# A one-layer decoder kernel: early gates, top-16 steps, piecewise reads, V's first block and the last run rearranged

## The chip, the cores and the metric

The kernel runs on one core of a Trainium2 chip. The core has a matmul engine (TensorE, PE in the profile, with its weight loads as PEld), a vector engine (DVE), an activation engine (ACT), GpSimd (POOL) and a queue engine (SP). DMAs are issued from SP and POOL here. Each engine works through its own list of instructions in order and waits on semaphores. The metric is the device time of one execution in microseconds (us). A profile is one execution with the hardware profiler on; its span runs from the first to the last instruction, and the execution's own time is a little longer.

## The reference

One decoder layer on 256 tokens of width 2048, in f32: two kinds of attention side by side, attention into 256 memory tokens, a layer of single-neuron experts chosen by product keys (PEER), and a last RMS norm. The change touches the PEER layer and the last norm:

```python
def peer_ffn(hn, w_pq, sub_keys, u_tab, v_tab):
    q = (hn @ w_pq).reshape(T, PEER_HEADS, 2, PEER_D_KEY // 2)      # 8 heads, 2 halves of 128
    s = jnp.einsum('thpd,hpkd->thpk', q, sub_keys)                  # 128 keys per half
    top_s, top_i = lax.top_k(s, 16)
    cand = top_s[:, :, 0, :, None] + top_s[:, :, 1, None, :]
    best_s, best_c = lax.top_k(cand.reshape(T, PEER_HEADS, 256), 16)
    expert = ia * 128 + ib                                          # one of 16384
    gate = jax.nn.softmax(best_s, axis=-1)
    a = jnp.einsum('td,ted->te', xt, u_tab[expert])
    hidden = gate * jax.nn.gelu(a)
    return jnp.einsum('te,ted->td', hidden, v_tab[expert])
...
h = h + peer_ffn(rmsnorm(h, norm_ffn), ...)
y = rmsnorm(h, norm_final)
```

## The kernel before

**Precision.** A weight tile `raw` (128 x 1024, 512 KB, four buffers) comes in over SP. ACT rounds it to `hi` and DVE computes the rest, `lo` (`parts`, L71 and L73). A block of weights (`fm_block`) is two such halves; for each PE runs 8 matmuls with `hi` and 8 with `lo`.

**Order.** The program is written in Python as one long list. A planner then orders each engine's instructions by a simulated time line, so an instruction can move ahead of others where its inputs seem ready. `add_manual_dep` ties an instruction behind another; `self.last_lo` is the latest `lo` in program order.

**Queries (`peer`).** For 8 heads, two weight blocks each (numbered 0 to 15 as `2 * h + p2`) give the queries. `sk`, a head's sub keys, are read over SP, `whole`, the tokens in f32, over POOL from the scratch tensor `hres` ahead of the loop; ACT scales `whole` and DVE norms it in four pieces (blocks 5 to 13). The last query block uses `whole` itself.

**Top-16 steps.** For each head and each half of 128 tokens, `topk_pieces` makes three steps (`keys`; `pairs` and `gate`; `ids` and `sums`), 48 in all. The third appends 16 table writes to `puts` (L1009): POOL scatters 128 gates at a time into a dense table of 128 x 128 x 256 gates in DRAM. Six steps are popped in the query loop. The others are popped beside chunks of U, one a chunk, but none at chunk 0 and at every fifth (`while pieces`). `some(4)` issues up to four waiting writes after each query block or chunk.

**U chunks.** 128 chunks of 128 experts each: PE multiplies, `join` adds the two halves, ACT applies gelu. A chunk's result lies in `self.buf` (`hb`). Chunks from `first` on multiply their gates at once (L814); their gates are read into `hb` eight chunks at a time. For the earlier ones gates are read later, four chunks at a time, into a tile `gates` that takes one of the four `raw` buffers (`table_read`, L797); DVE multiplies one chunk on (L757) and counts signs (L824). A read of the table waits for all table writes. `end` is the chunk at which the last write is placed; the early reads begin at `end + 5`, one a chunk.

**Lists and V.** Experts with one token, few tokens or many are told apart by the counts; ranks within a class are matmuls with small 0/1 matrices (`lists`: `totals` L854, `ranks` L862 and L863); POOL writes hidden rows into lists in DRAM (L892). This is done in two parts (chunks 0 to 83, and the rest). `v_phase` runs over 88 blocks of 128 listed experts: POOL gathers their rows of V (L1060), `hi` and `lo` are made as above (`scaled`, L80 and L82, for experts of one token), and `products` (L1089) adds into `out[tb][q]`, eight PSUM banks: two halves of 128 tokens, four column blocks. `plan` mixes wide blocks (FEW, ALL) with thin ones (ONE) into five runs. A FEW block has 12 matmuls, an ALL block 24, a ONE block 8. After the third run comes a rarely taken branch (`rest`, L1254), then the fourth run (one ALL block) and the last.

**The end.** `square` (L1208) sums squares of a column block, `gained` (L1212) multiplies it with the last gain, `root` takes the inverse root (L163 to L168, L1216, L1217) and `finish` scales (L1227, L1229) and stores. For the first half of the tokens these stand as steps in the last run, for the second behind it.

Of the kernel before, what the change touches and what calls it, by code (L numbers as in the profile page):

```python
# [28 lines left out]
D = 2048  # L29
# [23 lines left out]
class Layer:  # L53
# [595 lines left out]
    def peer(self):  # L649
        nc, tc, a = self.nc, self.tc, self.a  # L650
        with ExitStack() as es:
# [3 lines left out]
            self.total = [ba.tile([128, 128], F32, name="total%d" % tb) for tb in range(2)]  # L655
# [4 lines left out]
            self.listing = False  # L660
# [7 lines left out]
            with ExitStack() as e2:  # L668
                ps = self.ps = e2.enter_context(tc.tile_pool(name="ups", bufs=2, reuse_waits="tile", space=bass.MemoryType.PSUM))
                pieces = []  # L670
                with tc.tile_pool(name="tk", bufs=1, reuse_waits="tile") as tk:
# [9 lines left out]
                    for q in range(4):  # L681
                        xs = slice(q * 4, q * 4 + 4)
                        nc.gpsimd.dma_start(whole[:, xs, :], self.hres[:, xs, :])
                    normed = 0
                    for h in range(8):
                        sk = tk.tile([128, 2, 128], F32, tag="sk", name="sk", bufs=8)
                        nc.sync.dma_start(sk, a["subkeys"][:, 2 * h:2 * h + 2, :])
# [4 lines left out]
                        for p2 in range(2):  # L692
# [8 lines left out]
                            pq.append(q)  # L701
                            if 2 * h + p2 in (5, 7, 9, 11):
                                for k in range(4 * h - 8 + 2 * p2 - 2, 4 * h - 8 + 2 * p2 + 2):
                                    nc.scalar.activation(whole[:, k, :], whole[:, k, :], AF.Copy,
                                                         scale=self.gs[:, 3, k:k + 1])
                            if 2 * h + p2 in (7, 9, 11, 13):
# [5 lines left out]
                            elif 2 * h + p2 in (3, 4, 6, 8, 10, 12):  # L712
                                pieces.pop(0)()
# [114 lines left out]
    def lists(self, part, pool, tag, bufs):  # L828
# [21 lines left out]

        def totals(src, k):
            p = pool.tile([128, 4, 128], F32, tag=tag, name="ps_tot", bufs=bufs)
            for j in range(k):
                nc.tensor.matmul(p[:n, j, :], src[:, j, :], self.ones_b, start=True, stop=True)  # L854
# [163 lines left out]
    def plan(self):  # L1018
# [48 lines left out]
    def v_phase(self):  # L1067
# [6 lines left out]
        with ExitStack() as es:  # L1074
# [5 lines left out]
            def bank(tb):  # L1080
                ps = es.enter_context(psum("vps%d" % tb))
                out.append([ps.tile([128, 512], F32, name="out%d%d" % (tb, q)) for q in range(4)])

            def products(tb, hf, passes, last=False):

                first = not started[tb][hf]
                for n, (h, v) in enumerate(passes):
                    for q in range(2):
# [15 lines left out]
            def begin(first, n):  # L1104
# [276 lines left out]
```

## Time and profile before

| | |
|---|---|
| median of 3 runs | 1720.01 us (1719.34 to 1721.84) |
| the profiled execution, its own time | 1713.88 us |
| its span | 1712.1 us |
| mean granted clock of TensorE | 0.985 |
| busy: PE, PEld | 1637.2 us, 1388.0 us |
| busy: DVE, ACT, POOL | 1245.9 us, 1002.2 us, 748.8 us |
| queries begin, U's chunks begin, V begins | some 542, 640 and 1395 us into the span |

The page gives each engine's busy time and the span in 40 slices of 42.8 us. A timeline row has start, duration, engine, line, operation, the tiles written and read, their shapes and a count; the brackets hold the idle time before it and what ended it. A row of the waits has who waited for whom, the sum, the number of waits and the longest. A row of the windows has start:end, the length, then busy time and instructions of PE, PEld, DVE, ACT and POOL, the granted clock, the DMA share and GB/s. A grouped row has busy time and mean ns, then idle time and its releasers. `SPq` is SP's DMA queue; a row of it covers issues from the first to the last.

### The profile page before, as it was taken

The numbers are of one execution on the slowest core, as the hardware profiler recorded it, in microseconds if no ns is written. First come the engines' busy times: TensorE is split into PE (matmuls) and PEld (weight loads), VectorE is DVE, ScalarE is ACT, GpSimd is POOL, SyncE is SP. The second block draws the span as 40 slices with busy tenths as digits, with TensorE's granted clock in tenths as the row PEclk, the third lists the DMA queues.
The fourth block names the chain that finished last, engine by engine and source line by source line (L and its number), as shares of the span: only waits on it lengthen the run. The fifth ranks groups of instructions, "written<-read, shape, count | busy, mean of one in ns | idle before, by whom it ended". The sixth has DMA issues, their size and how long they took to land. (4 is left out here: it accounts for less than half of the span.)

```text
span 1712.1 us, 25608 instructions
## 1 busy us (share of the span) xinstructions
PE 1637.2 (96%) x8834; PEld 1388.0 (81%) x8834; DVE 1245.9 (73%) x2237; ACT 1002.2 (59%) x1483; POOL 748.8 (44%) x649
## 2 busy tenths in 40 slices
PE   7999999999999999999999957999999999999996
PEld 6888787888888788888888856888888877777874
DVE  5935475556668777999999928887566579788686
ACT  6534455676566546666666526665555466667575
POOL 6500002211115072888888871101777216786520
PEclk9999999999999999999999988999999999999998
DMA  8658459875656765666665637886889977998991
GB/s 285 224 187 292 165 197 364 316 237 194 217 161 186 236 187 179 188 181 189 174 196 175 189 83 264 301 283 214 248 270 257 413 260 261 406 405 311 415 367 64
DMA packets 139866, 417.01 MB, mean 244 GB/s; under 512 B 39177, under 2 KB 52105, under 8 KB 128208
## 3 DMA queue, kind: packets, MB, share of 16 engines
q1 hardware_dynamic: 97424, 254.21, 46.6%
q0 software_dynamic: 42304, 161.09, 24.9%
q8 instruction: 71, 1.16, 0.3%
q14 instruction: 67, 0.55, 0.1%
HBM read 371.36 MB, written 49.65 MB: 246 GB/s over the span
## 5 line engine op out<-in xcount | busy, mean ns | idle before, releaser
L73 DVE TENSOR_TENSOR lo<-raw,hi 128x1024 fp32r<-128x1024 f32 x434 | 534.3, 1234 | 261.2 <-ACT hi L71 244.3
L71 ACT ACTIVATE hi<-raw 128x1024 fp32r<-128x1024 f32 x438 | 462.8, 1058 | 419.0 <-issue 166.5
L89 PE MATMUL acc<-pair_f,hi 128*128 128x512 f32 x2288 | 578.5, 395 | 33.4 <-ACT hi L71 33.4
L89 PEld LDWEIGHTS acc<-pair_f,hi 128*128 128x128 f32 x2288 | 413.5, 190 | 109.5 <-ACT hi L71 34.8
L1009 POOL DMA_INDIRECT table<-total,place x256 | 325.8, 1273 | 147.2 <-issue 74.0
L91 PEld LDWEIGHTS acc<-pair_f,lo 128*128 128x128 f32 x2288 | 311.9, 190 | 22.4
L91 PE MATMUL acc<-pair_f,lo 128*128 128x256 f32 x2288 | 319.2, 282 | 0.0
L892 POOL DMA_INDIRECT rows<-hb,where x128 | 150.0, 1172 | 55.2 <-issue 34.1
L1060 POOL DMA_INDIRECT vrows<-V,index x88 | 117.2, 1331 | 86.4 <-DVE lo L73 31.2
L82 DVE SCALAR_TENSOR_TENSOR lo<-vrows,val,hi 128x1024 fp32r<-128x1024 f32 x96 | 122.8, 1282 | 34.8 <-ACT hi L80 27.1
L80 ACT ACTIVATE hi<-vrows,val 128x1024 fp32r<-128x1024 f32 x96 | 109.2, 1148 | 62.0 <-PE out L1089 33.7
L89 PE MATMUL acc<-pair_x,hi 128*128 128x512 f32 x512 | 131.9, 396 | 0.0
L73 DVE TENSOR_TENSOR lo<-vrows,hi 128x1024 fp32r<-128x1024 f32 x80 | 97.8, 1222 | 22.2 <-PE out L1089 8.4
L89 PEld LDWEIGHTS acc<-pair_x,hi 128*128 128x128 f32 x512 | 91.5, 189 | 16.5 <-issue 0.7
L71 ACT ACTIVATE hi<-vrows 128x1024 fp32r<-128x1024 f32 x80 | 84.3, 1054 | 33.4 <-PE out L1089 24.7
L1089 PE MATMUL out<-hi,ha 128*128 128x512 f32 x256 | 80.8, 406 | 7.1 <-PEq L1254 3.0
L1089 PE MATMUL out<-hi,hb 128*128 128x512 f32 x256 | 82.6, 406 | 2.2 <-issue 1.4
L1089 PE MATMUL out<-lo,ha 128*128 128x512 f32 x256 | 76.8, 405 | 0.0
L91 PEld LDWEIGHTS acc<-pair_x,lo 128*128 128x128 f32 x512 | 70.0, 190 | 6.4 <-DVE lo L73 1.6
L91 PE MATMUL acc<-pair_x,lo 128*128 128x256 f32 x512 | 73.8, 284 | 0.4 <-DVE lo L73 0.4
L89 PE MATMUL acc<-pair_o,hi 128*128 128x512 f32 x256 | 64.7, 393 | 0.9 <-DVE pair_o L589 0.9
L1089 PEld LDWEIGHTS out<-hi,ha 128*128 128x128 f32 x256 | 47.3, 190 | 22.1 <-ACT hi L71 5.8
(392 smaller groups left out, 2208.0 us busy)
## 6 DMA issues: line engine op xcount, KB each, us to landing
raw<-U SPq DMA_DIRECT2D x256, 512.0 KB, 4.4
table<-zero POOLq DMA_DIRECT2D x16, 1024.0 KB
raw<-w_sb SPq DMA_DIRECT2D x32, 512.0 KB, 6.1
raw<-w_out SPq DMA_DIRECT2D x32, 512.0 KB, 4.4
raw<-w_pq SPq DMA_DIRECT2D x32, 512.0 KB, 4.3
listed<-rows SPq DMA_DIRECT2D x88, 129.0 KB, 7.3
rows<-zero POOLq DMA_DIRECT2D x10, 1032.0 KB
gates<-table POOLq DMA_DIRECT2D x20, 512.0 KB
```

Source lines behind the costliest of these rows:

```text
L71: nc.scalar.activation(hi, raw, AF.Copy)
L73: self.last_lo = (eng or nc.vector).tensor_tensor(out=lo, in0=raw, in1=hi.bitcast(F32), op=ALU.subtract)
L80: nc.scalar.activation(hi, raw, AF.Copy, scale=val)
L82: self.last_lo = nc.vector.scalar_tensor_tensor(lo, raw, val, hi.bitcast(F32), op0=ALU.mult, op1=ALU.subtract)
L89: mm(ps, hi[:, n * m:(n + 1) * m], pair[:, k, :], start=first and n == 0, stop=False)
L91: mm(ps[:, T:], lo[:, n * m:(n + 1) * m], pair[:, k, :T], start=False, stop=last and n == len(ks) - 1)
L892: ins = nc.gpsimd.indirect_dma_start(out=self.rows[part], out_offset=bass.IndirectOffsetOnAxis(ap=where[:, i - lo:i - lo + 1], axis=0), in ...
L1009: ins = self.nc.gpsimd.indirect_dma_start(out=self.table, out_offset=bass.IndirectOffsetOnAxis(ap=self.place[tb][:, s:s + 1], axis=0), in_ ...
L1060: ins = nc.gpsimd.indirect_dma_start(out=raw, out_offset=None, in_=self.a["V"], in_offset=bass.IndirectOffsetOnAxis(ap=self.index[part, cl ...
L1089: mm(out[tb][hf * 2 + q], h, v[:, q * 512:(q + 1) * 512], start=first and n == 0, stop=last and n == len(passes) - 1)
```

## The change

- **Top-16 steps.** Nine steps are popped in the query loop, not six (blocks 2, 3, 4, 5, 6, 8, 10, 12, 14).
- **Early gates.** The early reads begin at `end + 9`.
- **Tokens and sub keys.** `whole` is read in four pieces after blocks 1, 3, 5 and 7, and `sk` over POOL head by head, each tied behind the latest `lo`.
- **V's first block.** Two of V's PSUM banks have a place of their own from the start of `peer`, the others come one by one; the first block is opened ahead of the second lists, and its hidden pair lies in the old `total` tiles.
- **Ranks.** The rank matmuls and the one of `excess` are tied behind the latest `lo`.
- **Last run.** It holds six blocks FEW1 (three of each part) instead of three FEW1 and three ONE1. The last block's second half of products is kept back and done column block by column block between `square` and `gained`. `root` is shortened: the square root takes scale and bias on ACT, and a factor -0.5 moves into `gained`. Scaling and storing of the first half of the tokens is spread: two column blocks in the run, two on ACT behind the second half's square root.

```diff
-            self.total = [ba.tile([128, 128], F32, name="total%d" % tb) for tb in range(2)]
+            self.total = [ba.tile([128, 128], F32, tag="total%d" % tb, name="total%d" % tb) for tb in range(2)]
...
+            self.banks = []
+            for q in range(2):
+                p = es.enter_context(tc.tile_pool(name="vps0%d" % q, bufs=1, reuse_waits="tile", side="right",
+                                                  space=bass.MemoryType.PSUM))
+                self.banks.append(p.tile([128, 512], F32, name="out0%d" % q))
...
-                    for q in range(4):
-                        xs = slice(q * 4, q * 4 + 4)
-                        nc.gpsimd.dma_start(whole[:, xs, :], self.hres[:, xs, :])
...
-                        nc.sync.dma_start(sk, a["subkeys"][:, 2 * h:2 * h + 2, :])
+                        ins = nc.gpsimd.dma_start(sk, a["subkeys"][:, 2 * h:2 * h + 2, :])
+                        if h:
+                            tc.add_manual_dep(ins.ins, self.last_lo.ins.name, SYNC, reason="beside its block")
...
+                            if 2 * h + p2 in (1, 3, 5, 7):
+                                xs = slice(4 * h + 2 * p2 - 2, 4 * h + 2 * p2 + 2)
+                                ins = nc.gpsimd.dma_start(whole[:, xs, :], self.hres[:, xs, :])
+                                tc.add_manual_dep(ins.ins, self.last_lo.ins.name, SYNC, reason="beside its block")
...
+                            if 2 * h + p2 in (2, 3, 4, 5, 6, 8, 10, 12, 14):
+                                pieces.pop(0)()
...
-                            elif 2 * h + p2 in (3, 4, 6, 8, 10, 12):
-                                pieces.pop(0)()
...
-                    if c >= end + 5 and early:
+                    if c >= end + 9 and early:
...
+        def beside(ins):
+            tc.add_manual_dep(ins.ins, self.last_lo.ins.name, SYNC, reason="beside a block")
...
-                nc.tensor.matmul(p[:n, j, :], src[:, j, :], self.ones_b, start=True, stop=True)
+                beside(nc.tensor.matmul(p[:n, j, :], src[:, j, :], self.ones_b, start=True, stop=True))
...
-                nc.tensor.matmul(p[:, j, :n], self.before, src[:, j, :], start=True, stop=False)
+                beside(nc.tensor.matmul(p[:, j, :n], self.before, src[:, j, :], start=True, stop=False))
...
-                      ((0, ONE0, 5, a[ONE0]), (0, ONE1, 0, a[ONE1]), (0, FEW1, 0, a[FEW1]), (0, ALL, 0, a[ALL])),
-                      ((1, ONE0, 0, b[ONE0]), (1, ONE1, 0, b[ONE1] - 3), (1, FEW0, 0, b[FEW0]), (1, ALL, 0, b[ALL] - 1)),
+                      ((0, ONE0, 5, a[ONE0]), (0, ONE1, 0, a[ONE1]), (0, FEW1, 3, a[FEW1]), (0, ALL, 0, a[ALL])),
+                      ((1, ONE0, 0, b[ONE0]), (1, ONE1, 0, b[ONE1]), (1, FEW0, 0, b[FEW0]), (1, ALL, 0, b[ALL] - 1)),
                       ((1, ALL, b[ALL] - 1, b[ALL]),),
-                      ((1, ONE1, b[ONE1] - 3, b[ONE1]), (1, FEW1, 0, b[FEW1]))):
+                      ((1, FEW1, 0, b[FEW1]), (0, FEW1, 0, 3))):
...
-            at, ahead, turn = [0], [len(self.sets)], [0]
+            at, ahead, turn = [0], [10], [0]
...
+            own = [self.ba.tile([128, 128], F32R, tag="total%d" % j, name="own%d" % j) for j in range(2)]
+            opened[0] = begin(*self.bundles[0], own)
...
-                nc.vector.tensor_mul(og[tb][:, cs], out[tb][q], gain[:, cs])
+                nc.vector.scalar_tensor_tensor(og[tb][:, cs], out[tb][q], -0.5, gain[:, cs],
+                                               op0=ALU.mult, op1=ALU.mult)
...
+                nc.vector.tensor_reduce(out=s, in_=z[tb], axis=AX.X, op=ALU.add)
+                at = nc.scalar.activation(t, s, AF.Sqrt, scale=1.0 / D, bias=eps)
+                nc.vector.tensor_scalar(v, s, 1.0 / D, EPS, op0=ALU.mult, op1=ALU.add)
+                nc.vector.reciprocal(y, t)
+                nc.vector.tensor_scalar(u, y, y, v, op0=ALU.mult, op1=ALU.mult)
+                nc.vector.scalar_tensor_tensor(u, u, 3.0, y, op0=ALU.subtract, op1=ALU.mult)
...
             for q in range(4):
+                if q > 1:
+                    products(1, 1, kept, True, (q - 2,))
                 square(1, q)
                 gained(1, q)
-            finish(1, root(1))
+            y, at = root(1)
+            for q in (2, 3):
+                finish(0, ys[0], q, nc.scalar, at)
+            for q in (3, 0, 1, 2):
+                finish(1, y, q, nc.scalar if q == 3 else nc.vector)
```

More of the change, by code (lines that the diff above doesn't have):

```diff
@@ L1080, in bank, with products @@
             def bank(tb):
-                ps = es.enter_context(psum("vps%d" % tb))
-                out.append([ps.tile([128, 512], F32, name="out%d%d" % (tb, q)) for q in range(4)])
-            def products(tb, hf, passes, last=False):
+                out.append(self.banks if tb == 0 else [])
+                for q in range(len(out[tb]), 4):
+                    ps = es.enter_context(psum("vps%d%d" % (tb, q)))
+                    out[tb].append(ps.tile([128, 512], F32, name="out%d%d" % (tb, q)))
+            def products(tb, hf, passes, last=False, qs=(0, 1)):
                 first = not started[tb][hf]
                 for n, (h, v) in enumerate(passes):
-                    for q in range(2):
+                    for q in qs:
                         mm(out[tb][hf * 2 + q], h, v[:, q * 512:(q + 1) * 512], start=first and n == 0,
@@ L1101, in hidden_pair, with begin @@
                 return hh, hl
[L1104 removed]
+            def begin(first, n, into=None):
                 t = self.st.tile([128, 4 * W], F32, tag="raw", name="listed", bufs=RAW)
@@ L1138, in half, with run @@
                     hh, hl = x[:, tq], y[:, tq]
-                    products(tb, hf, ((hh, vh), (hl, vh), (hh, vl)), left[tb][hf] == 0)
+                    passes = ((hh, vh), (hl, vh), (hh, vl))
+                    if kept is None:
+                        products(tb, hf, passes, left[tb][hf] == 0)
+                    else:
+                        kept.extend(passes)
             opened = {}
-            at, ahead, turn = [0], [len(self.sets)], [0]
-            def run(upto, beside=[], steps=[], split=None):
+            at, ahead, turn = [0], [10], [0]
+            def run(upto, beside=[], steps=[], split=None, kept=None):
                 while at[0] < self.ends[upto]:
@@ L1178, in excess @@
                     tot = cps.tile([128, 2], F32, name="ps_over")
-                    nc.tensor.matmul(tot, self.ones, self.over, start=True, stop=True)
+                    ins = nc.tensor.matmul(tot, self.ones, self.over, start=True, stop=True)
+                    tc.add_manual_dep(ins.ins, self.last_lo.ins.name, SYNC, reason="beside a block")
                     for part in range(2):
@@ L1218, in root @@
[L1218 to L1230 removed]
+                small = lambda tag: vw.tile([128, 1], F32, tag=tag, name=tag, bufs=2)
@@ new lines, in root, with finish @@
+                return u, at
+            def finish(tb, y, q, eng, after=None):
+                cs = slice(q * 512, (q + 1) * 512)
+                if eng is nc.scalar:
+                    ins = nc.scalar.activation(og[tb][:, cs], og[tb][:, cs], AF.Copy, scale=y)
+                    if after is not None:
+                        tc.add_manual_dep(ins.ins, after.ins.name, SYNC, reason="the root first")
+                else:
+                    nc.vector.tensor_scalar_mul(og[tb][:, cs], og[tb][:, cs], y)
+                nc.sync.dma_start(a["out"][tb * 128:(tb + 1) * 128, cs], og[tb][:, cs])
@@ L1232, in v_phase @@
             og = [fin[:, 3, :], fin[:, 0, :]]
             z = [vw.tile([128, 4], F32, tag="fz", name="fz", bufs=2) for _ in range(2)]
-            ends = [(lambda q=q: [square(0, x) for x in q]) for q in ((0,), (1,), (2, 3))]
-            ends += [lambda: (gained(0, 0), gained(0, 1)), lambda: (gained(0, 2), gained(0, 3))]
-            ends += [lambda: finish(0, root(0))]
-            run(4, steps=ends)
+            eps = vw.tile([128, 1], F32, tag="fe", name="fe", bufs=1)
+            nc.vector.memset(eps, EPS)
@@ L1238, in v_phase @@
+            ys = []
+            ends = [lambda: (square(0, 0), square(0, 1)), lambda: (square(0, 2), square(0, 3)),
+                    lambda: ys.append(root(0)[0]), lambda: (gained(0, 0), gained(0, 1)),
+                    lambda: (gained(0, 2), gained(0, 3)),
+                    lambda: (finish(0, ys[0], 0, nc.vector), finish(0, ys[0], 1, nc.scalar))]
+            kept = []
+            run(4, steps=ends, kept=kept)
             assert not ends
             for q in range(4):
+                if q > 1:
+                    products(1, 1, kept, True, (q - 2,))
```

24 lines of the change are left out of this document (5 added, 19 removed).

## The prediction

> **What bounds the kernel now.** I read the page's slices first, to see whether one engine fills the span.
>
> ```profile
> PE   7999999999999999999999957999999999999996
> DVE  5935475556668777999999928887566579788686
> PEclk9999999999999999999999988999999999999998
> ```
>
> TensorE (PE) is busy nine tenths nearly everywhere, so a shorter kernel means shorter holes in PE. One hole stands out, in slices 24 and 25 of 42.8 us each, where the clock drops too. The waits of PE name its size, and PE's timeline its place:
>
> ```profile
> PE acc L89 <- ACT hi L71: 33.4, 7, 24.8
> ```
>
> ```profile
> 998.43 2.00 PE L89 MATMUL acc<-pair_f,hi 128*128 128x512 f32 x8
> 1001.23 2.00 PE L89 MATMUL acc<-pair_f,hi 128*128 128x512 f32 x8
> 1006.50 2.11 PE L89 MATMUL acc<-pair_f,hi 128*128 128x512 f32 x8 [2.32 <-ACT hi L71]
> 1037.17 3.44 PE L89 MATMUL acc<-pair_f,hi 128*128 128x512 f32 x8 [24.81 <-ACT hi L71]
> ```
>
> A half block of U starts every 2.80 us, so a chunk costs PE 5.6 us. Then come holes of 2.32 and 24.81 us, and the first eight matmuls afterwards take 3.44 instead of 2.00. The timelines of DVE and POOL show who was late:
>
> ```profile
> 1006.48 2.36 DVE L73 TENSOR_TENSOR lo<-raw,hi 128x1024 fp32r<-128x1024 f32 x2 [1.43 <-ACT hi L71]
> 1033.76 2.48 DVE L757 TENSOR_TENSOR hb<-hb,gates 128x1024 f32<-128x1024 f32 x2 [24.91 <-DMA gates<-table]
> ```
>
> ```profile
> 671.71 0.98 POOL L1009 DMA_INDIRECT table<-total,place  x1 [30.45 <-DVE total L989]
> 1026.88 0.98 POOL L1009 DMA_INDIRECT table<-total,place  x1 [0.30 <-issue]
> 1029.75 1.24 POOL L797 DMA_DIRECT2D gates<-table  x2 [1.88 <-issue]
> ```
>
> ```profile
> L1009 POOL DMA_INDIRECT table<-total,place x224 | 288.2, 1287 | 98.4 <-issue 64.6 <-DVE total L989 30.5 <-DMA table<-total,place 1.5
> ```
>
> DVE is through at 1008.84 and stands before the first early multiply, which needs gates read from the table. That read must follow all 256 table writes, and POOL finishes them at 1027.86. The row of the grouped view (671.7 to 1028) says why: after one idle of 30.5 us POOL issues 224 writes back to back, (1027.86 - 671.71) / 224 = 1.59 us each. So the hole is set by when this chain starts, 671.71, and how many writes it holds.
>
> **The change part by part.** *Top-16 steps and early gates.* The schedule is counted from the code. There are 48 steps; the third step of a head and token half releases 16 writes. Before, 6 run in the queries and 42 beside chunks (none in chunk 0, four in five after), which ends after 53 chunks; 24 writes, six chunks' worth, are then left: `end` is 59, first early read at 59 + 5 = 64. After, 9 and 39 give 49 chunks, `end` 55, and the read at 55 + 9 = 64 again. So the read does not move, while the writes before it do. Three groups of 16 now leave within the queries instead of two; POOL idled 30.45 us there, so the third group costs it nothing (without that idle, 16 x 1.59 = 25 us). The chunk stage starts with the same step positions, so the chain starts at 671.71 with 208 writes: 208 x 1.59 = 331 us, end 1002.4. From the last write's end to the gates' use were 1033.76 - 1027.86 = 5.9 us, so they are there at 1008.3, where DVE asks at 1008.84. If an earlier part shortens the queries, both shift alike. I count 24.8 of hole plus 1.4 of slow matmuls, less 1.5 in reserve because the margin is 0.5 us: **-24.7**. I keep the 2.32 hole, as two gates tiles still hold two of the four `raw` buffers meanwhile. Bounds: all of it, -28.5; at writes of 1.65 us, 12 us late, -12.7. The three added steps run on DVE, seven tenths busy in the queries by the slices. A window there holds most of one group's steps beside two weight blocks' work:
>
> ```profile
> 570.00:586.00 16.00, 11.81 (x59) 9.88 (x58) 11.02 (x35) 7.71 (x9) 0.00 (x0) 0.89 0.79 239
> ```
>
> So a group is under 11 us of DVE, and without idle there PE would wait at most that long.
>
> `first` falls from 80 to 72: the early multiplies (now 18, chunks 65 to 82) lie beside chunks that are gated themselves. The windows, the grouped rows and DVE's timeline:
>
> ```profile
> 1050.00:1072.00 22.00, 22.00 (x127) 19.35 (x126) 21.48 (x26) 15.04 (x24) 2.65 (x5) 1.00 0.88 310
> ```
>
> ```profile
> L824 DVE TENSOR_REDUCE count<-signs 128x4 f32<-128x512 bf16 x8 | 5.4, 679 | 0.0
> ```
>
> ```profile
> 1135.86 0.42 DVE L814 TENSOR_TENSOR hb<-hb,ut 128x256 f32<-128x256 f32 x1
> ```
>
> DVE is 98% busy there (21.48 of 22), but catching up after the hole. Four chunks' work in 22 us would be 5.4 us a chunk; a gated chunk adds 0.42 and half a reduce, 0.34: 6.2 against PE's 5.6, over ten chunks 6 us. Without the catch-up it fits. Between 0 and 6 I take **+1.5**, nearer to nothing since PE lost nothing in that window.
>
> *Tokens and sub keys.* PE, ACT, SP's queue and POOL at the hole in the queries:
>
> ```profile
> 578.15 5.52 PE L89 MATMUL acc<-pair_f,hi 128*128 128x512 f32 x16 [4.00 <-ACT hi L71]
> 585.41 2.00 PE L89 MATMUL acc<-pair_f,hi 128*128 128x512 f32 x8
> ```
>
> ```profile
> 577.04 1.06 ACT L71 ACTIVATE hi<-raw 128x1024 fp32r<-128x1024 f32 x1 [6.01 <-DMA raw<-w_pq]
> ```
>
> ```profile
> 554.51 5.35 SPq L791 DMA_DIRECT2D hb<-number  x2
> 559.91 4.81 SPq L687 DMA_DIRECT2D sk<-subkeys  x1
> 571.29 27.21 SPq L62 DMA_DIRECT2D raw<-w_pq  x13
> ```
>
> ```profile
> 552.15 2.10 POOL L683 DMA_DIRECT2D whole<-hres  x4
> ```
>
> A weight was late because SP stood in issues of 5.35 and 4.81 us ahead of it, while 2 MB of tokens moved. The edit takes sub keys off SP, and spreads tokens over blocks 1 to 7. The hole is 4.00; two halves took 7.26 (578.15 to 585.41) instead of 5.6, another 1.7. The `number` issues stay on SP, so I leave 1 us: **-4.7**, between -5.7 and +1 (a scale of tokens that waits on ACT). On POOL 12 issues, 2.10 / 4 = 0.5 us each, now stand between table writes, in its idle. The added waits on a `lo` hold the writes queued behind them; that is a rival below.
>
> The Trainium skill's page "DMA: Bandwidth & Descriptors", section "Issuing engines are not separate DMA queues", says that all queues feed the same 16 engines and that another issuer saves only issue time, usually small; here the trace shows one issue of 4.81 us, so the issue time was not small.
>
> *V's first block and tied ranks.* PE's timeline and the window of the first run:
>
> ```profile
> 1395.83 0.50 PE L1089 MATMUL out<-hi,ha 128*128 128x512 f32 x1 [1.03 <-ACT ha L1099]
> 1397.07 0.93 PE L1089 MATMUL out<-hi,ha 128*128 128x512 f32 x3 [0.73 <-DVE ut L125]
> 1398.78 1.05 PE L1089 MATMUL out<-lo,ha 128*128 128x512 f32 x2
> 1402.07 0.63 PE L1089 MATMUL out<-lo,ha 128*128 128x512 f32 x2
> 1423.18 0.23 PE L854 MATMUL ps_tot<-ones_b,both 128*44 128x128 bf16 x1 [2.11 <-DVE both L873]
> 1424.42 0.38 PE L1179 MATMUL ps_over<-over,ones 128*128 128x2 f32 x2 [0.88 <-DVE over L886]
> ```
>
> ```profile
> 1395.00:1428.00 33.00, 27.48 (x106) 19.63 (x107) 29.20 (x68) 21.43 (x31) 13.88 (x12) 0.91 0.95 372
> ```
>
> Own banks and own `ha`, `hb` take away 1.03 + 0.73; the ties put PE's rank products behind ready work, against 2.11 + 0.88. After the first pair of holes two matmuls took 1.05 instead of 0.63. But DVE is busy 29.20 of 33 and none of its work goes, so at most 3.8 us fall out unless DVE starts earlier. I take **-3**, between +1 (a tie that holds ranks too long) and -6.
>
> The Trainium skill's page "TensorE: Matmul & The Clock Gate", section "Why this matters for your kernels", asks only that idle gaps stay under some 3 us; by it the holes of 1.03 and 0.73 cost no clock, and this sum would be about 1 us smaller. The 1.05 behind them disagrees.
>
> *New last run.* A group of V's products, the window from the branch on, then the tail on PE and DVE:
>
> ```profile
> L1089 PE MATMUL out<-hi,ha 128*128 128x512 f32 x256 | 80.8, 406 | 7.1 <-PEq L1254 3.0
> ```
>
> ```profile
> 1676.90:1701.90 25.00, 23.21 (x84) 17.07 (x84) 20.77 (x35) 17.16 (x29) 0.00 (x0) 0.86 0.08 23
> ```
>
> ```profile
> 1701.17 0.70 PE L1089 MATMUL out<-lo,listed 128*128 128x512 f32 x2
> ```
>
> ```profile
> 1702.27 1.27 DVE L1229 TENSOR_SCALAR fin<-fin,fy 128x512 f32<-128x512 f32 x3
> 1703.45 1.28 DVE L1212 TENSOR_TENSOR fin<-out,fin 128x512 f32<-128x512 f32 x2
> 1704.65 0.15 DVE L1216 TENSOR_REDUCE fv<-fz 128x1 f32<-128x4 f32 x1
> 1706.22 1.28 DVE L1229 TENSOR_SCALAR fin<-fin,fy 128x512 f32<-128x512 f32 x3
> ```
>
> 84 matmuls become 96. A pair takes 0.63 above and a single one 0.41 by its group, so each adds 0.22: 2.6 us come here and leave earlier runs, and PE's total stays. A block of the kind that moves in brings 12 matmuls per two `lo`, the kind that moves out 8, so DVE holds PE up less here: -0.5. After PE's end at 1701.87 DVE still did three scalings of the first half and two products (1702.27 to 1704.65) before the sum; now they lie earlier or on ACT, and the sum waits for one square: some 1.6 earlier. The root, 1.57 us, loses two small steps, 0.4. Together **-2.5**, between +1 and -5.
>
> Three blocks of the first part leave the second run too, so the second part's first fetch comes three blocks sooner and finds about two list writes more still to be issued, 3.2 us at the table writes' 1.59. I cost it at nothing: some 14 blocks are fetched ahead by then, of 8 matmuls and 1.8 us or more each, 25 us. Without that cover it is 3.2 us, inside the +1 to -5 with the other terms. The first part's lists start one chunk sooner, beside U chunks; nothing waits for them there.
>
> The sum: -24.7 + 1.5 - 4.7 - 3 - 2.5 = -33.4. The span 1712.1 becomes 1678.7. The profiled execution took 1713.88, the runs' median is 1720.01; I carry the difference over: 1720.0 - 33.4 = **1686.6**.
>
> **The rivals.** Where the last head's queries stand, on PE (the last of its two weight blocks):
>
> ```profile
> 633.34 7.07 PE L118 MATMUL acc<-whole,raw 128*128 128x256 f32 x32
> ```
>
> *The queues buy nothing*: the weights are late through shared engines, not through SP, and the 4.00 hole stays: 1691.3. For it: tokens and `number` still move; against: the 4.81 issue. *The writes slow down*: POOL's writes take 1.65 us as more transfers share the early stretch; 12 us return: 1698.6. Against: the chain's DVE neighbours are the same. *The change does not do what it says*: the third group does not leave in the queries, the chain still ends at 1027.86, and PE, 4.7 earlier, waits as much longer: only the last two parts pay, 1720.0 + 1.5 - 3 - 2.5 = 1716. *Slower*: the token and sub-key transfers wait for a `lo` in POOL's in-order queue, and the planner has put the writes of all three groups behind the last of them, at the last head's first block, 633.34 - 5.6 = 628. Then 48 + 208 writes x 1.59 = 407 us end at 1035, gates 1041, a hole of 37 instead of 25; 12 lost and the overlap's 1.5 against the queries' 4.7 make +9 with the V parts at nothing: 1729. It decides from first writes behind 620 on. For it: each wait blocks what stands behind it; against: the first group is ready before most of those transfers.
>
> **How the numbers follow.** Forecast 0.66 (1686.6), queues 0.10 (1691), slow writes 0.12 (1699), not done 0.05 (1716), slower 0.07 (1729). The range 1676 to 1704 takes in the first three: its low end has the gates' part at -28.5, V at -6, the tail at -5; its high end the slow writes with the overlap's 6. Within 0.2% of the time before, 3.4 us, a measurement here cannot tell a change: faster 0.90, same 0.03, slower 0.07.
>
> **What would show it.** Right: POOL's last table write near 998 (5 earlier through the queries); the first early multiply without a wait of over 3 us; no hole over 2 us in the queries; PE at half clock only around the branch; the sum of squares within 1.5 us of PE's last matmul. Wrong: a chain that starts later than 672, holes on `hi` between chunks 72 and 82, or PE waiting on `whole`'s scaling.

## The result

The time went from 1719.34 us (median of 11 runs, 1715.89 to 1731.68) to 1708.67 (11 runs, 1706.04 to 1714.95). The ratio is 0.9932, with a 95% interval of 0.9911 to 0.9953: faster, by a third of what was forecast (1686.6, range 1676 to 1704). The profiled execution took 1706.04, its span 1704.1 against 1712.1. In two of the groups of runs below the U chunks were stretched, by some 65 to 120 us in the profiles; their totals are compared only within the group, and every kernel of them but one (the reads four chunks earlier) was run again in another group.

The slices on the page of the kernel after, of 42.6 us each:

```profile
PE   7999999999999999999999969999999899999996
DVE  6935475556668988999999638886665578777786
PEclk9999999999999999999999979999999999999998
```

One hole, formerly spread over slices 24 and 25, is in slice 24 now (6 for PE, 7 for the clock), and slice 32, U's last chunks, is thinner (8). Four rows of PE's waits over the whole span: the first holds the hole; the second and the last are in V, behind slice 32; the third has 4.3 of its 6.2 us, in six waits, in slice 32:

```profile
PE acc L91 <- DVE lo L73: 15.8, 5, 14.3
...
PE out L1101 <- ACT hi L80: 6.7, 4, 2.7
PE acc L89 <- ACT hi L71: 6.2, 7, 2.0
PE ps_tot L864 <- DVE both L883: 3.5, 1, 3.5
```

Then PE's, DVE's and POOL's timelines of the kernel after at the hole of 14.3:

```profile
991.56 2.00 PE L89 MATMUL acc<-pair_f,hi 128*128 128x512 f32 x8
1007.82 2.07 PE L91 MATMUL acc<-pair_f,lo 128*128 128x256 f32 x8 [14.25 <-DVE lo L73]
1009.69 3.62 PE L89 MATMUL acc<-pair_f,hi 128*128 128x512 f32 x8
```

```profile
1005.40 1.23 DVE L764 TENSOR_TENSOR hb<-hb,gates 128x1024 f32<-128x1024 f32 x1 [20.60 <-DMA gates<-table]
```

```profile
998.80 0.98 POOL L1019 DMA_INDIRECT table<-total,place  x1 [0.30 <-issue]
1001.65 0.57 POOL L804 DMA_DIRECT2D gates<-table  x1 [1.87 <-issue]
```

The last table write ended at 999.78, 28 us earlier than before; that was forecast ("near 998"). The gates were there at 1005.4. But DVE asked for them at 1005.40 - 20.60 = 984.8, not at 1008.84. The wait ended 28.4 us earlier than before and began 24.0 earlier, so it is only 4.3 shorter (20.60 instead of 24.91).

Where the 8.0 us of span came from, stage by stage, in the two profiles (a chunk's start is that of its first matmul):

| stage | before | after | change | forecast |
|---|---|---|---|---|
| up to the queries' first matmul | 541.50 | 540.81 | -0.7 | 0 |
| queries, to chunk 0 | 98.56 | 92.90 | -5.7 | -4.7 |
| chunk 0 to chunk 66 (the hole) | 404.13 | 391.91 | -12.2 | -24.7 |
| chunk 66 to chunk 84 | 100.53 | 104.43 | +3.9 | +1.5 |
| chunk 84 to U's last matmul | 250.08 | 252.86 | +2.8 | 0 |
| U's last matmul to the span's end | 317.28 | 321.19 | +3.9 | -5.5 |

Two steps carry the miss: the hole (12.5 short) and V with the tail (9.4; this stage differs by more than its 3.9 between profiles of one and the same V part, as shown below).

### The profile page after: what moved, and what is told of

The parts are those of the page before. It is cut to its first block, busy times and chain, and to the rows that moved or that the text cites. A ratio compares the mean times of both kernels' runs of the same rounds, so it can differ in the third digit from the quotient of the medians.

```text
span 1704.1 us, 25608 instructions
## 1 busy us (share of the span) xinstructions
PE 1636.5 (96%) x8834; PEld 1388.5 (81%) x8834; DVE 1245.0 (73%) x2238; ACT 1000.1 (59%) x1483; POOL 761.7 (45%) x656
## 5 line engine op out<-in xcount | busy, mean ns | idle before, releaser
L91 PE MATMUL acc<-pair_f,lo 128*128 128x256 f32 x2288 | 321.2, 283 | 15.1 <-DVE lo L73 15.1
L1070 POOL DMA_INDIRECT vrows<-V,index x88 | 125.0, 1421 | 84.8 <-DVE lo L73 55.2
L82 DVE SCALAR_TENSOR_TENSOR lo<-vrows,val,hi 128x1024 fp32r<-128x1024 f32 x96 | 122.9, 1283 | 42.2 <-ACT hi L80 33.4
L71 ACT ACTIVATE hi<-vrows 128x1024 fp32r<-128x1024 f32 x80 | 84.0, 1053 | 30.4 <-PE out L1101 19.1
```

The lines of the kernel that those rows point to most:

```text
L71: nc.scalar.activation(hi, raw, AF.Copy)
L82: self.last_lo = nc.vector.scalar_tensor_tensor(lo, raw, val, hi.bitcast(F32), op0=ALU.mult, op1=ALU.subtract)
L91: mm(ps[:, T:], lo[:, n * m:(n + 1) * m], pair[:, k, :T], start=False, stop=last and n == len(ks) - 1)
L1070: ins = nc.gpsimd.indirect_dma_start(out=raw, out_offset=None, in_=self.a["V"], in_offset=bass.IndirectOffsetOnAxis(ap=self.index[part, cl ...
```

## Experiments on the hole

Theory A: the program's order on DVE sets the hole. The first early multiply stands there among the `lo` passes of the U chunks, two to a chunk; DVE works in order, so where it stands is when DVE asks. The passes can be counted in the traces. First the kernel before, then the kernel after, each from the queries' start to its first early multiply (count, durations in ns, first and last start):

```profile
L73 DVE TENSOR_TENSOR lo<-raw,hi x159: 1201/1219/1751, 540.6 to 1007.6; 128x1024 fp32r<-128x1024 f32 x159
```

```profile
L73 DVE TENSOR_TENSOR lo<-raw,hi x155: 1202/1219/1755, 539.9 to 983.6; 128x1024 fp32r<-128x1024 f32 x155
```

Four passes fewer in the kernel after: two chunks, 11.2 us at 2.80 a pass. In the kernel before these four took longer, since they stood in holes before `hi`: 17.2 us, from the end of the 304th pass at 991.67 to 1008.84. The other 6.9 of the 24.0 were there ahead of the 304th pass already, 6.4 of them at chunk 0. Theory B: the gates tiles, which hold `raw` buffers, starve U's loads whatever DVE does. Theory C: only POOL's last write counts.

**The reads four chunks later, alone.** In the kernel before:

```
-                    if c >= end + 5 and early:
+                    if c >= end + 9 and early:
```

> The kernel before with only the early reads four chunks later, no more top-16 steps in the queries. The first early multiply stands behind 312 lo passes instead of 308. Theory A: DVE asks 4 x 2.80 = 11.2 us later while the last write stays near 1027.9, so the hole of 24.8 shrinks to about 13.6, chunk 66 starts near 1033 instead of 1044, about 1707 (0.9935): the four chunks alone are worth what the kernel after gained in this stage. Theory C: the last write stays and so does the hole's end; 1718.

Measured: 1712.09 (1708.85 to 1716.55), ratio 0.9942 with an interval of 0.9920 to 0.9963. DVE's and PE's timelines of this kernel:

```profile
1033.53 1.23 DVE L757 TENSOR_TENSOR hb<-hb,gates 128x1024 f32<-128x1024 f32 x1 [20.81 <-DMA gates<-table]
```

```profile
1035.94 2.08 PE L91 MATMUL acc<-pair_f,lo 128*128 128x256 f32 x8 [14.45 <-DVE lo L73]
```

The hole is 14.45 (13.6 expected) with a last write at 1027.71. It lies behind the start of chunk 66 now, which comes at 1013.90 (1033 expected); at chunk 84 the kernel is 10.6 us ahead of the kernel before, and the time is 5 above the 1707 expected. The kernel after has 14.25 with a last write at 999.78. So against this kernel the 28 us by which the chain ends earlier (16 writes fewer, and a start 1.3 us earlier) were worth nothing at the hole: DVE's question moved as far forward, from 1033.53 - 20.81 = 1012.72 to 984.8, as the writes did.

**The multiply moved, the reads not.** In the kernel after, the multiply is tied behind the last `lo` of its chunk:

```
-                        nc.vector.tensor_mul(d, d, t)
+                        ins = nc.vector.tensor_mul(d, d, t)
+                        self.tc.add_manual_dep(ins.ins, self.last_lo.ins.name, SYNC, ...)
```

> The kernel after, with each early multiply tied behind the last lo pass of the chunk beside which it is written. It stands on DVE behind 310 lo passes instead of 304. Theory A (the planner's order on DVE set the hole): DVE asks near 984.8 + 6 x 2.80 = 1001.6, the gates land at 1005.4, the PE hole of 14.3 before chunk 64 falls to at most 2, the start of chunk 66 moves from 1025.6 to about 1010, the whole to about 1696 (0.986 of before). Theory B (the gates tiles hold two of the four raw buffers): a hole of 8 or more stays, in front of ACT's hi; 1704 or more. Theory C (only POOL's last write counts): 1708.

Measured: 1742.39 (1738.71 to 1745.86), ratio 1.0121, interval 1.0077 to 1.0165: slower than before the change. DVE asked at 1001.86 (1001.6 expected) and the first hole shrank to 5.99, but then one came in nearly every chunk; PE's waits over the span:

```profile
PE acc L89 <- ACT hi L71: 43.8, 23, 6.0
```

Theories A and B both had a part. The later place on DVE took 8 us off the hole of 14.25; but a gates tile that is read and then waits for its multiply keeps one of the four `raw` buffers. Here POOL issued three reads from 1006.21 to 1007.54, and their multiplies came at 1010.43, 1018.19 and 1029.29; in the kernel after each of the first five reads was followed by its multiply, 3.8 to 4.8 us later, before the next read was issued. That this is why U's halves came late fits theory B and the next run. Reads and multiplies must move together.

**Reads and multiplies three chunks later.** In the kernel after:

```
-                    if c >= end + 9 and early:
+                    if c >= end + 12 and early:
```

> The kernel after with the early reads, and with them the early multiplies, three chunks later (read at chunk 67 instead of 64). The first early multiply stands on DVE behind 310 lo passes instead of 304. Theory A (the planner's order): DVE asks near 984.8 + 6 x 2.80 = 1001.6, the gates land near 1005.4, the hole of 14.3 falls to at most 2 and, as reads and multiplies move together, none of the holes of the tied run (1.4 to 6.0 in every chunk) appears; chunk 66 starts near 1010, the whole near 1694 (0.985 of before). Theory B (gates tiles take raw buffers from U's loads as soon as they are read): chunks 67 to 84 take 7 to 8 us as in the tied run, above 1720.

Measured: 1693.73 (1688.57 to 1695.81), ratio 0.9845, interval 0.9808 to 0.9883. DVE and PE of this kernel:

```profile
1009.78 1.23 DVE L764 TENSOR_TENSOR hb<-hb,gates 128x1024 f32<-128x1024 f32 x1 [8.44 <-DMA gates<-table]
```

```profile
1012.20 1.21 PE L91 MATMUL acc<-pair_f,lo 128*128 128x256 f32 x8 [2.09 <-DVE lo L73]
1013.25 3.36 PE L89 MATMUL acc<-pair_f,hi 128*128 128x512 f32 x8
1016.40 1.41 PE L91 MATMUL acc<-pair_f,lo 128*128 128x256 f32 x8
```

DVE asked at 1001.34 (expected 1001.6), the hole is 2.09 (at most 2 expected) and the time is within 1 us of the expected 1694. Chunk 66 starts at 1008.1 (near 1010 expected), 17.5 earlier than in the kernel after; the hole lies behind this point now, and at chunk 84 the lead is 13.1. No hole of the tied run's series is there: from chunk 66 to 84 it takes 108.9 us, the tied kernel 153.4, so theory B's times do not come. Theory C falls: the last write, at 1003.48, was 3.7 later than in the kernel after, and the hole was 12 us smaller.

**The reads four chunks earlier.** In the kernel after:

```
-                    if c >= end + 9 and early:
+                    if c >= end + 5 and early:
```

> The kernel after with the early reads where the old rule puts them (five chunks behind the last released write, chunk 60). The first early multiply stands behind 300 lo passes. Theory A: DVE asks 4 x 2.80 = 11.2 us earlier than in the kernel after, the hole grows from 14.3 to about 25.5, time about 1720: the four chunks are then worth 11 and the three more top-16 steps by themselves nothing in this stage. Theory C: no change against the kernel after, 1708.

Measured: 1803.67 against 1812.85 for the kernel before in its group (0.9865, interval 0.9809 to 0.9921). With U's chunks stretched, the writes ended early enough beside them and DVE waited 1.26, so the size of the hole was not tested. The place was: 300 passes, and the first two multiplies stand together there, as they do in the kernel before.

**Only the place, no step moved.** In the kernel before:

```
-                    if c >= end + 5 and early:
+                    if c >= end + 11 and early:
```

> The kernel before with only the early reads six chunks later (chunk 70); six top-16 steps in the queries as before. The first early multiply stands on DVE behind 316 lo passes, 4 more than with four chunks (1712.1, hole of 14.45). Theory A (the multiply's place sets the hole): the hole falls to about 3, and without a single earlier table write the gates part is worth 22 to 25; with less than 5 us lost at U's end, 1700 to 1703. Theory T (lists and V's first fetches, two chunks later, no longer fit before V): what the hole gives is lost before V's first matmul, 1709 to 1712.

Measured: 1709.44 (1699.22 to 1715.39), ratio 0.9938, interval 0.9914 to 0.9962. Two rows of PE:

```profile
1039.30 2.08 PE L91 MATMUL acc<-pair_f,lo 128*128 128x256 f32 x8 [5.01 <-DVE lo L73]
...
1383.51 0.79 PE L1089 MATMUL out<-hi,ha 128*128 128x512 f32 x1 [6.96 <-ACT ha L1099]
```

The hole falls to 5.01 (some 3 expected), as theory A says, and the time is theory T's. The loss is not all in front of V: against the kernel before this profile is 19.1 us ahead at chunk 84, 18.3 at U's end, 12.3 at V's first product, behind the hole of 6.96, and 8.6 at the end. So this is what the three earlier top-16 steps buy: in this stage not a shorter wait, but room behind the early multiplies: 18 reads from chunk 67 end at chunk 84, 20 from chunk 70 at chunk 89, and the lists and V's fetches come after them (the first rows of V are fetched at 1298.7 with reads at chunk 67 in the kernel after, at 1340.6 here).

All places together (passes counted in the traces from the start of the program):

| kernel | first read at chunk | `lo` passes ahead | DVE waits | PE's hole |
|---|---|---|---|---|
| before | 64 | 308, two multiplies there | 24.91 | 2.32 + 24.81 |
| before, reads 4 later | 68 | 312 | 20.81 | 14.45 |
| before, reads 6 later | 70 | 316 | 11.36 | 5.01 |
| after | 64 | 304 | 20.60 | 14.25 |
| after, reads 3 later | 67 | 310 | 8.44 | 2.09 |

By the kernels with one multiply at its place, the place is 176 + 2 x chunk. The kernel before should then have 304; it has 308 and two multiplies at once. There the planner, which orders DVE by its own time line, held the first multiply back by two chunks. Why is argued, not shown: in its time line the writes ended too late for 304, and with the writes earlier the hold was gone. (The kernel with reads at chunk 60 has 300 and two multiplies, where the rule gives 296.) The other regularity is in the last columns: DVE's wait less PE's hole is 6.35 or 6.36 in the four kernels with one multiply waiting. PE runs on through finished halves for 8.8 us past DVE's question, and starts again 2.4 after the gates are there (the multiply, then a `lo`). In the kernel before, where two multiplies waited, it ran on for only 3.5, started again 3.4 behind, and 24.91 of waiting cost 27.1; that the two gates tiles held two of the four `raw` buffers is the likely reason, not a tested one.

The numbers hold in other profiles too: the four kernels below with the early gates of the kernel after ask at 984.6 to 985.5 and have holes of 14.3 to 16.8, and the three below with reads at chunk 67 ask at 1001.3 to 1001.7, two with holes of 2.1 and 2.3 and one, whose gates were there 2 us sooner, with none at this place.

## Experiments on the other parts

**Sub keys back on SP's queue**, tokens still spread:

```
-                        ins = nc.gpsimd.dma_start(sk, a["subkeys"][:, 2 * h:2 * h + 2, :])
...
+                        nc.sync.dma_start(sk, a["subkeys"][:, 2 * h:2 * h + 2, :])
```

The tie behind `last_lo` goes too.

> The kernel after with the sub keys' eight loads back on SP's queue; the tokens stay spread over blocks 1 to 7. The queries took 98.6 us before (541.5 to 640.1) and 92.9 after. Theory L (the sub keys' issues of 4.8 us on SP made the weights late): the queries take 96 to 98.5, a hole of 2 to 4 on hi is back. Theory M (2 MB of tokens at once made both the issues long and the weights late): the queries stay at 93 to 94 and no issue of a sub key takes over 3 us.

Measured: 1708.12 (0.9918, interval 0.9893 to 0.9942); the queries took 93.6. SP's issues in its queries, and all of PE's waits there:

```profile
556.00 2.88 SPq L688 DMA_DIRECT2D sk<-subkeys  x1
```

```profile
PE acc L89 <- ACT hi L71: 0.3, 1, 0.3
```

Theory M: the longest sub-key issue is 2.88 instead of 4.81, and the hole of 4.00 stays away although SP issues them. With the sub keys back on SP, the spread of the tokens is the only transfer that the edit still moves in the queries: it did it. The sub keys' queue was worth some 0.7 (93.6 against 92.7 to 92.9 in the kernels with the sub keys on POOL).

**V's first block without its own banks and pair**: the own PSUM banks, the own `ha` and `hb` and the early opening are taken out:

```
-            own = [self.ba.tile([128, 128], F32R, tag="total%d" % j, name="own%d" % j) for j in range(2)]
-            opened[0] = begin(*self.bundles[0], own)
```

> The kernel after without own banks and own hidden pair of V's first block; the ties stay. From the end of U's last matmul to the 100th product of V the kernel before took 36.4 us, the kernel after 36.7, other kernels with the change's V part 37.6 to 38.3. Theory J (run 0 is bound by DVE's work on the lists, so that an earlier start only meets later holes): the hole at the start is back at 1 to 3 us, the holes of 1.38 and 1.47 behind it are smaller, the stretch takes 36 to 38, the time is the same as the kernel after within 3. Theory K (the own block is worth what its holes were, 1.8, and something else in the change costs the same): the stretch takes 38.5 to 40.

Measured: 1709.66 (0.9932, interval 0.9910 to 0.9955). From U's last matmul to V's 100th product: 36.2, against 36.7 in the kernel after and 37.8 to 39.9 in seven other kernels with the own block. First the kernel after, then this one, PE at V's start:

```profile
1388.89 1.18 PE L1101 MATMUL out<-hi,ha 128*128 128x512 f32 x4 [1.38 <-ACT ha L1111]
1391.55 0.73 PE L1101 MATMUL out<-hi,hb 128*128 128x512 f32 x2 [1.47 <-DVE f L854]
```

```profile
1387.67 0.74 PE L1097 MATMUL out<-hi,ha 128*128 128x512 f32 x2 [1.03 <-ACT ha L1107]
1388.90 0.71 PE L1097 MATMUL out<-hi,ha 128*128 128x512 f32 x2 [0.50 <-DVE ut L125]
```

Theory J: with the own block the holes of 1.03 and 0.50 are gone at the first block, and holes of 1.38 and 1.47 are there at the second, whose `ha` and `hb` come no earlier.

**Ranks and overflow untied.** In the kernel after, for the sums and the ranks (the overflow's tie goes likewise):

```
         def beside(ins):
-            tc.add_manual_dep(ins.ins, self.last_lo.ins.name, SYNC, ...)
+            pass
```

> The kernel after without the ties of the list ranks' and the overflow's matmuls. From V's first matmul to the 100th product the kernel before took 35.4 us, the kernel after 36.9, with a hole of 3.47 before ps_tot where before had 2.11. Theory F (the tie makes the longer wait: PE passes ready work later): the 3.47 hole goes back to about 2, run 0 takes 35.5. Theory G (DVE is simply behind with the sums that ps_tot needs, tied or not): the hole stays above 3, no change that can be measured, 1708.

Measured: 1711.20 (0.9931, interval 0.9910 to 0.9953). PE at the list's sums, of this kernel:

```profile
1414.49 0.23 PE L864 MATMUL ps_tot<-ones_b,both 128*44 128x128 bf16 x1 [3.47 <-DVE both L883]
```

3.47 with the ties and 3.47 without: they do nothing for this wait. Theory G: DVE is late with `both`.

**The old lists of runs** in the kernel after, with nothing kept for the end:

```
-                      (... (0, FEW1, 3, a[FEW1]), ...),
+                      (... (0, FEW1, 0, a[FEW1]), ...),
...
-                      ((1, FEW1, 0, b[FEW1]), (0, FEW1, 0, 3))):
+                      ((1, ONE1, b[ONE1] - 3, b[ONE1]), (1, FEW1, 0, b[FEW1]))):
...
-            run(4, steps=ends, kept=kept)
+            run(4, steps=ends)
```

> The kernel after with the old lists of runs: three FEW1 blocks of the first part back in run 1, the old last run of three wide and three thin blocks, nothing kept for the end. From V's first matmul to PE's end the kernel before took 306.0 us, the kernel after 310.3. Theory D (the new mix in run 1, 17 wide beside 27 thin blocks, cost it 7.4 us of holes in front of ACT's hi): the holes of 1.34, 2.38, 1.44 and 2.69 go, the last run gives back its 3.6, the stage takes about 306.5, 1704. Theory E (the holes come from V's rows that land late, whatever the mix): the stage takes 312 to 314, the time is 1710 to 1712.

Measured: 1709.03 (0.9926, interval 0.9904 to 0.9948); from V's first matmul to PE's end 309.8 (306.0 before, 310.3 after). Neither theory's number came. In run 1, PE waited 5.3 us for ACT's `hi` of thin blocks with the old mix and 6.7 with the new one, so the mix isn't what opened these holes; and its last run, 84 matmuls, took 22.9 us where the kernel before had 25.0 and the kernel after, with 96, has 24.2; so part of the 3.6 that the expectation counts as the new last run's gain was the one profile of before. What opens them is not settled.

**All of V's edits away**, the rest kept with reads at chunk 67: the kernel before with the change's queries, whole, and one line:

```
-                    if c >= end + 5 and early:
+                    if c >= end + 12 and early:
```

> The kernel before with the change's queries (nine top-16 steps, tokens and sub keys spread) and its early reads, these three chunks later still (chunk 67); V's part, ties, plan and tail as before. The same kernel with the change's V part took 1693.7 (0.9845 of before). From U's end to the span's end the profiles of kernels with the old V part took 316.3 to 321.2, those with the new one 315.8 to 321.4. Theory N (V's edits together are worth nothing that can be measured): 1691 to 1696. Theory P (they cost 4 to 5 us): about 1689. Theory Q (they gain the forecast 5.5): about 1699.

Measured: 1689.25 (1684.88 to 1692.15), ratio 0.9828, interval 0.9803 to 0.9854. It has the lowest ratio here, though the intervals of all kernels with reads at chunk 67 overlap, and theory Q is out. Beside it in the same group, with V's edits and one tie more in the tail:

```
+                        if len(qs) == 1 and n == 0:
+                            tc.add_manual_dep(ins.ins, ended[0].ins.name, SYNC, ...)
```

> The kernel after with the early reads three chunks later and the last block's kept products tied behind all products of the first half. In a profile of it the sum of squares began 1.9 us after PE's end instead of 2.4, since the four products of DVE (2.87) begin with the first square and stand before the sum; PE's end to the span's end took 10.40 instead of 11.03. Expected: the same tail, 10.2 to 10.6, and a time that cannot be told from 1693.7 without the tie (1691 to 1696).

Measured: 1691.58 (1685.37 to 1695.40), ratio 0.9835, interval 0.9798 to 0.9872. The ranges overlap, so N (V's edits do nothing) and P (they cost a few us) are not told apart. The tail took 10.69 (10.2 to 10.6 expected); a sum of squares 1.3 to 1.6 earlier and 9.4 to 9.8 to the end, which I had first expected of this tie, did not come. From U's last matmul to the span's end, seven profiles with the whole new V part have 315.8 to 321.4, three with the old one 315.9 to 321.2 (left out is the one whose lists came too late for V): the stage differs from profile to profile by more than the 3.9 between before and after.

**The gates of more chunks late**: with `end + 12`, the chunks up to 80 instead of 72 ("the last kernel" below is the one with reads and multiplies three chunks later).

```
-                first = (end + 16 + GROUP - 1) // GROUP * GROUP
+                first = (end + 24 + GROUP - 1) // GROUP * GROUP
```

> As the last kernel, and the chunks up to 80 instead of 72 get their gates late (20 early multiplies instead of 18), so that fewer early multiplies lie beside chunks that are gated themselves. In the kernel after, chunks 66 to 84 took 104.4 us, 3.9 above 18 x 5.59. Theory H (the overlap overloads DVE): the 3.9 falls to at most 1.5, 1 to 2 us below the last kernel. Theory I (these holes come from the lists and the counts that start there, later now): no difference, or up to 3 slower since the lists start four chunks later and end nearer to V.

Measured: 1692.18 (1690.99 to 1694.33), ratio 0.9835, interval 0.9797 to 0.9873. It is 1.7 ahead at chunk 84 and 0.5 at chunk 120. Inconclusive: H's size at the first place, nothing left at the second.

## Why the prediction failed, step by step

**Queries (-4.7, came -5.7): right in size, wrong in cause.** I put the 4.00 hole to SP's issues, the sub keys' above all. The run with them on SP shows that the hole came from 2 MB of tokens moving at once; the long sub-key issue went with it. My rival "the queues buy nothing" had this cause, but not that spreading the tokens would remove the hole. The Trainium skill's page "DMA: Bandwidth & Descriptors", section "Issuing engines are not separate DMA queues", which I had weighed and set aside, says that another issuer saves only issue time, usually small: the 0.7 measured for the sub keys' queue agrees with it.

**The chain (last write near 998, came 999.78): right.** 208 writes began at 669.12, 1.59 us each. What the forecast did not say: there is no idle left ahead of them, all 256 writes run on from 591.41, so a fourth group would not come for nothing any more.

**Early gates (-24.7, came -12.2): the step that failed is one sentence, "the read does not move", and its use of 1008.84.** I took the time at which DVE asked before for the time at which it would ask after, because the read stays at chunk 64. What is fixed at chunk 64 is the read's place in the code. The multiply's place on DVE is the planner's, and in the kernel before the late writes had pushed it two chunks back. Two multiplies in one row (x2 at 1033.76, which I quoted) were the trace's sign of it: one read per chunk should give one multiply per chunk (that the planner held the first one is argued, as said above). With the right place the same arithmetic holds: gates at 1005.4 less an ask at 984.8, less the 6.35 of the table, gives the 14.25. The sign of being right that I named ("the first early multiply without a wait of over 3 us") failed, with 20.60, and showed it at once.

That half of the term came all the same is luck. Of the 12.9 us by which PE's holes shrank (27.13 to 14.25), only 4.3 are a shorter wait of DVE, which is what the term was about. The other 8.6 are the finished halves on which PE ran on (6.35 against 0.10 in the kernel before) and the hole of 2.32, which I had kept in the sum and which went.

**Overlap (+1.5, came +3.9): too small.** The bound of 6 covered it; what part is DVE's load and what part the lists is not settled. **Chunk 84 to U's end (+2.8)** was in no term, and I made no experiment on it. The traces place it: from chunk 84 to 120 nothing changed (202.19, now 202.11), and the rest grew from 47.89 to 50.76, with six waits for `hi` of 4.3 us together instead of three of 2.0. With V's old part and reads at chunk 67 the rest takes 49.14, so V's edits are not the whole of it. Why `hi` is late there is open.

**V's first block and ties (-3, came nothing): the term was mis-sized.** The text said that DVE has 29.20 of 33 us to do and that none of it goes away; it then took 3 us for holes all the same. The holes moved to the next block, whose `ha` and `hb` are no earlier, and `ps_tot` waits for DVE with a tie or without one.

**Last run and tail (-2.5): the mechanism was half right, and its transfers were left out.** The forecast was a sum of squares within 1.5 us of PE's last matmul. DVE's timeline of the kernel after, with PE's end at 1693.07:

```profile
1692.66 2.85 DVE L1232 SCALAR_TENSOR_TENSOR fin<-out,fin 128x512 f32<-128x512 f32 x4 [1.34 <-ACT fin L1228]
1695.43 0.14 DVE L1239 TENSOR_REDUCE fs<-fz 128x1 f32<-128x4 f32 x1
```

It came 2.36 after, behind all four products with the gain; before, it was 2.78. So 0.4 was gained, not 1.6; the root itself became 0.36 shorter (1.57 to 1.21), about as forecast. And PE's end to the span's end grew from 10.21 to 11.03 (four profiles of the old tail have 10.18 to 10.22, seven of the new one 10.31 to 11.18). Two of the first half's scalings, moved behind the root, took their stores with them. The DMA engines' busy tenths and traffic from PE's end to the span's end, first before, then after:

```profile
DMA  0000399999999995000000799999999991000000
GB/s 0 0 0 0 104 368 392 377 360 400 385 392 360 392 392 184 24 0 0 0 0 0 280 376 376 369 408 337 408 384 377 384 368 32 0 0 0 0 0 0
```

```profile
DMA  0010000000000000899999999999998200000000
GB/s 0 0 30 0 0 0 0 0 0 0 0 0 0 0 0 0 319 401 364 386 356 372 409 349 371 386 386 394 372 401 357 74 22 15 0 0 0 0 0 0
```

Before, four stores move while the sum is formed and four behind the root. After, the engines idle until the root is there, and then six stores of 256 KB are left. At some 380 GB/s a store takes 0.7 us, so two more behind the root are 1.4 by estimate, more than the 0.8 that the sum and the root had gained. The growth of 0.82 in this profile is not these stores alone: its last 0.8 us of traffic run at 74, 22 and 15 GB/s, and in the profile with 10.31 to the end the traffic stops without such a remainder. What the remainder is, is not settled. The tail's extra tie moved the sum from 2.36 to 1.91 and left the stores: 10.69 to the end.

**The rivals.** None of mine was this one. The nearest, slow writes at 1699, priced a later end of the wait, not an earlier beginning. In the sum, the 33.4 lacked one question: for each wait that ends earlier, does it still begin at the same time?

## What to carry to other kernels

Where a planner orders the instructions by its own time line, a wait has two ends that both move: making the awaited thing earlier can pull the waiting instruction forward by as much, so the waiter's place in its engine's order must be read again for the new program, or fixed by hand together with the transfer that feeds it. Two instructions of a regular series found side by side can be a sign that something held them. Count the stores that a moved step takes along: at the end of this kernel six stores weighed more than the arithmetic that was saved.

## What the hardware showed unexpectedly

A hole in PE has a price beyond its length, and most holes of some 2 us pay it already. Three holes of the tied kernel on PE's timeline, each followed by the eight matmuls of a half block, which take 2.00 undisturbed:

```profile
1023.82 3.33 PE L89 MATMUL acc<-pair_f,hi 128*128 128x512 f32 x8 [2.26 <-ACT hi L71]
1026.95 1.48 PE L91 MATMUL acc<-pair_f,lo 128*128 128x256 f32 x8
...
1044.70 3.67 PE L89 MATMUL acc<-pair_f,hi 128*128 128x512 f32 x8 [3.46 <-ACT hi L71]
...
1053.54 2.11 PE L89 MATMUL acc<-pair_f,hi 128*128 128x512 f32 x8 [1.42 <-ACT hi L71]
```

After 2.26 us the next matmuls lost 1.3 + 0.4 us (the `lo` ones took 1.48 instead of 1.11), after 3.46 also 1.7, after 1.42 only 0.1. Over the U chunks of 13 profiles, compared with 5.59 us for the next 32 matmuls: holes up to 1.7 us lost at most 1.0 and mostly under 0.6; of 17 holes from 1.87 to 2.9 us, 11 lost 1.4 to 1.8; every longer one lost 1.4 to 2.9, a hole of 24.81 no more than one of 2.5. The price is the granted clock: in the 3.2 us from 1023.8 it is 0.59 and in the 3.7 from 1044.7 it is 0.54, but 1.00 in the 2.5 from 1053.5; and behind four holes of 1.95 to 2.32 us in other profiles that lost at most 0.3, it is 1.00. So the length of a hole alone does not decide; what else does is open. The Trainium skill's page "TensorE: Matmul & The Clock Gate", section "Why this matters for your kernels", asks for gaps under some 3 us; here 11 of 17 holes between 1.87 and 2.9 us paid. Holes of 1.0 to 1.1 us lost 0.1 to 0.55, so the 0.42 that the prediction held against the page (1.05 instead of 0.63) is real, but small.
